# The delta rule's decay matrices: six tiles in the outputs' accumulators beside the pair of their own, in a hybrid attention layer

## The chip, the cores and the metric

The kernel runs on one core of a Trainium2 chip. The metric is device time in microseconds of one execution; the times of before are the median of three runs. Beside them stands one execution that was recorded by the hardware profiler. The kernel is written with a tile framework: tiles come from pools with a number of buffers each, the framework puts in the semaphore waits, and a scheduler that simulates the program (`schedule_with_timeline_sim=True`) decides in which order each engine gets its instructions. On the chip every engine then works through its list in that order.

## What is computed

One layer with 512 latent tokens and 256 context tokens, model width 1024: a half-step SwiGLU feed-forward block (FFN1), then two mixers side by side, neighbourhood attention with 8 heads of 64 and a bidirectional gated delta rule with 4 heads of 128, merged by gates, then a second feed-forward block (FFN2). The change is in the delta rule. Its core in the reference, for chunks of tokens:

```python
k, v, g, beta = chunk(k), chunk(v), jnp.cumsum(chunk(g), axis=-1), chunk(beta)
decay = jnp.exp(jnp.where(lower, g[..., :, None] - g[..., None, :], -jnp.inf))
k_beta = k * beta[..., None]
m = jnp.where(strict, jnp.einsum('...ik,...jk->...ij', k_beta, k) * decay, 0.0)
uw = lax.linalg.triangular_solve(jnp.eye(GDN_CHUNK, dtype=m.dtype) + m, rhs, left_side=True, lower=True, unit_diagonal=True)
...
# per chunk, state s:
v_new = u - w @ s;  s_next = s * g_tot + k_tail^T @ v_new
o = (q * exp(g)) @ s + ((q k^T) * decay) @ v_new
```

The decay matrix, the exponential of differences of a running sum, multiplies both products, k·k (before the triangular inverse) and q·k (for the outputs).

## The kernel before

The kernel works with chunks of 128 tokens: six steps `s` of the scan, of which 0 and 1 are the context's and 2 to 5 the latent tokens', in both directions at once. Two heads make a pair `p`, so a pair and a step hold four 128x128 matrices (two directions, two heads).

**Grams.** `gram(p, s, bd, g)` makes what one pair and step need. It takes a tile `Dt` of [128, 4, 128] (pool `gbase`, 2 buffers), loads the running sums `gcd` into it with one DMA from SyncE's queue (SP, L918), subtracts and masks with four instructions of VectorE (DVE, L921) and takes the exponential on ScalarE (ACT, L922). TensorE (PE) makes k·k in PSUM (`pq`, 2 buffers; every matmul of this part is issued by the helper at L857). Four DVE instructions make `Bt = pq * beta * Dt` (L927), and a DMA stores it to `bd` (L928). From step 2 on there is also the product q·k, from which DVE makes `At` (L931). For steps 4 and 5 the products come back from DRAM (`kq<-kqd`, L906), where steps 2 and 3 left them (L901, L902). The twelve grams are numbered here 0 to 11 in program order; four of them are a group, `grams(0)`, `grams(1)`, `grams(2)`.

**Inverses.** Behind each group stands `base_inverse`. It loads the diagonal 32x32 blocks of the group's sixteen matrices from `bd` (`Ltr` and `L`, L947; a copy on ACT, L948; a memset on GpSimd, L950), and inverts them in 31 steps, each a multiplication `bt` (L954) and a reduction into `Xt` (L955) on DVE. Here this is called the chain. Four DMAs write `Xt` to `rd` (L959). `inverse` reads these blocks back (`T<-rd`, L976), transposes them (L978, L979) and builds the inverses of 64x64 and 128x128 blocks with small matmuls (`pi`, L857). The scan's steps (`scan_step`) use them; from step 2 on they write the outputs to the accumulators `oacc0` and `oacc1`, one for each pair of heads, [128, 4, 2, 128] each (pool `gq`), which `gdn_out` reads at the end.

**Fill work.** Beside all this, PE has to multiply the latent tokens with further columns of `w_in`: matmuls into `pm` (L190 to L192, each weight split into `wh`, cast on ACT at L135, and `wl`, subtracted on DVE at L137, from `wr`, loaded at L172). Their results leave PSUM over ACT (`spill`, L605 to L609) and SP (L613). `turn` releases them at set rates behind the last matmul of the delta rule, by `tc.issue_after`. The attention that follows makes scores `sc` (L1240), transposes probabilities (`pt`, L1255), copies them on ACT (`pT`, L1257) and multiplies them with the values (`po`, L1266); the merge of the mixers fills PE in between, with `pm` matmuls as well.

The program order of the part that matters: some fill work, `grams(0)` with its chain, `grams(1)`, then the inverses of group 0 between the steps of group 1's chain, the scan's first steps, `grams(2)`, and so on.

Of the kernel before, what the change touches and what calls it, by code (L numbers as in the profile page):

```python
# [13 lines left out]
ALU = mybir.AluOpType  # L14
# [4 lines left out]
P = 128  # L19
# [39 lines left out]
def body(ctx, tc, I, out, dbg=None):  # L59
    nc = tc.nc  # L60
    V, S, G, T = nc.vector, nc.scalar, nc.gpsimd, nc.tensor
    dbg = dbg or {}

    def pool(name, side="left", space=None):
        kw = dict(name=name, bufs=1, reuse_waits="tile")
        if space is not None:
            kw["space"] = space
        else:
            kw["side"] = side
        g = tc.tile_pool(**kw)  # L70
        st = ExitStack()
        p = st.enter_context(g)
        return p, st.close
# [17 lines left out]
    ident = ident_t[:]  # L91
# [12 lines left out]
    def rsqrt_eps(sp, src, n, scale=None, eng=G):  # L104

        ve = tl(sp, [P, n], f"ve{n}", 4)
        if scale is None:
            marks["ve"] = eng.tensor_scalar(ve[:], src, EPS, None, op0=ALU.add).ins  # L108
        else:
            G.tensor_scalar(ve[:], src, scale, EPS, op0=ALU.mult, op1=ALU.add)  # L110
        rs = tl(sp, [P, n], f"rs{n}", 4)
        G.tensor_tensor(rs[:], ve[:], mhalf[:, 0:n], ALU.pow)  # L112
        return rs
# [508 lines left out]
    beta = tl(gd, [P, 2, 6, 4], "beta")  # L622
    gcum = tl(gd, [P, 2, 6, 4], "gcum")
# [223 lines left out]
    gq, close_gq = pool("gq")  # L847
    spool, done = [gq], [0]
    gb_, close_gb = pool("gbase", "right")
# [6 lines left out]
    def mm(*a, **k):  # L856
        last[0] = T.matmul(*a, **k).ins  # L857

    def mt(*a):
        last[0] = T.transpose(*a).ins  # L860
# [11 lines left out]
    def turn(kind, i):  # L872

        due[0] += RATE[kind][i]
        while due[0] >= 1:
            due[0] -= 1
            with tc.issue_after(last[0]):
                next(fills, None)

    def mats_of(s):  # L880
        return [(0, FWD_CH[s], 0), (0, FWD_CH[s], 1), (1, BWD_CH[s], 0), (1, BWD_CH[s], 1)]
# [6 lines left out]
    def products(p, s):  # L888
# [21 lines left out]
        if s >= 2:  # L910
            yield one(1, qT, 2)
            turn("g", s // 2)

    def gram(p, s, bd, g):

        mats = mats_of(s)
        Dt = tl(gb_, [P, 4, P], "Dt", 2)
        nc.sync.dma_start(Dt[:], bass.AP(gcd.tensor, gcd.offset + (4 * s + 2 * p) * P, [[0, P], [24 * P, 2], [1, 2 * P]]))  # L918
        for m, (d, c, i) in enumerate(mats):
            msk = cst[:, (C_MF if d == 0 else C_MB):][:, 0:P]  # L920
            V.scalar_tensor_tensor(Dt[:, m], Dt[:, m], gcum[:, d, s, 2 * p + i:2 * p + i + 1], msk, op0=ALU.subtract, op1=ALU.add)  # L921
        S.activation(Dt[:], Dt[:], AF.Exp)  # L922
        Bt, At = tl(gq, [P, 4, P], "Bt", NBT), None
        for n, t in enumerate(products(p, s)):
            if n == 0:
                for m, (d, c, i) in enumerate(mats):
                    V.scalar_tensor_tensor(Bt[:, m], t[m] if s == 1 else t[:, m], beta[:, d, s, 2 * p + i:2 * p + i + 1], Dt[:, m], op0=ALU.mult, op1=ALU.mult)  # L927
                nc.sync.dma_start(bass.AP(bd.tensor, bd.offset + g * MSTR, [[P, P], [4 * MSTR, 4], [1, P]]), Bt[:])  # L928
            else:
                At = tl(gq, [P, 4, P], "At", NAT)  # L930
                V.tensor_tensor(At[:], t[:], Dt[:], ALU.mult)  # L931
        return Bt, At
# [103 lines left out]
    def bc4(t, s, p):  # L1036

        return t[:, :, s, 2 * p:2 * p + 2, None].to_broadcast([P, 2, 2, P])

    def v4(t):  # L1040
        return t.rearrange("p (d i) c -> p d i c", d=2)

    oaccs = [tl(gq, [P, 4, 2, P], f"oacc{p}") for p in range(2)]

    def scan_step(p, s, Tt, At, Sst):
        cf, cb = FWD_CH[s], BWD_CH[s]
        mats = mats_of(s)
        oacc = oaccs[p]
        if Sst is not None:
            ks = tl(pgq, [P, 4, P], "pc", 2)  # L1050
            for m, (d, c, i) in enumerate(mats):
                mm(ks[:, m, :], kT[2 * p + i][:, c], Sst[:, m], start=True, stop=True)
            turn("s", s // 2)
            r = tl(gq, [P, 4, P], "r", 2)
            for m, (d, c, i) in enumerate(mats):
                V.scalar_tensor_tensor(r[:, m], ks[:, m], neg[:, d, s, 2 * p + i:2 * p + i + 1], vtok[2 * p + i][:, c], op0=ALU.mult, op1=ALU.add)
            rs = [r[:, m] for m in range(4)]
        else:
            rs = [vtok[2 * p + i][:, c] for (d, c, i) in mats]
        pv = tl(pgq, [P, 4, P], "pc", 2)  # L1060
        for m in range(4):
            mm(pv[:, m, :], Tt[m], rs[m], start=True, stop=True)
        turn("s", s // 2)
        vn = tl(gq, [P, 4, P], "vn", 2)
        V.tensor_tensor(v4(vn[:]), v4(pv[:]), bc4(beta, s, p), ALU.mult)
        Sn = None
        if s < 5:
            kt = tl(gq, [P, 4, P], "ktail")
# [12 lines left out]
        if s >= 2:  # L1081
            o1 = tl(pgq, [P, 4, P], "pc", 2)
            for m, (d, c, i) in enumerate(mats):
                mm(o1[:, m, :], qT[2 * p + i][:, c - 2], Sst[:, m], start=True, stop=True)
            turn("s", s // 2)
            ot = tl(gq, [P, 4, P], "otmp")
            V.tensor_tensor(v4(ot[:]), v4(o1[:]), bc4(eg, s, p), ALU.mult)
            o2 = tl(pgq, [P, 4, P], "pc", 2)
            for m in range(4):
                mm(o2[:, m, :], At[:, m], vn[:, m], start=True, stop=True)  # L1090
            turn("s", s // 2)
            if s < 4:
                V.tensor_tensor(oacc[:, cf - 2], ot[:, 0:2], o2[:, 0:2], ALU.add)
                V.tensor_tensor(oacc[:, cb - 2], ot[:, 2:4], o2[:, 2:4], ALU.add)
            else:
                V.tensor_tensor(ot[:], ot[:], o2[:], ALU.add)
                G.tensor_tensor(oacc[:, cf - 2], oacc[:, cf - 2], ot[:, 0:2], ALU.add)
                G.tensor_tensor(oacc[:, cb - 2], oacc[:, cb - 2], ot[:, 2:4], ALU.add)
        return Sn

    def gdn_out(p):

        oacc = oaccs[p]
        for t2 in range(2):
            o = oacc[:, 2 * t2:2 * t2 + 2].rearrange("p t i c -> p (t i) c")
            sq = tl(gq, [P, 4, P], "r", 2)
            S.activation(sq[:], o, AF.Square)
            ss = tl(gq, [P, 4], "ss", 2)
            V.tensor_reduce(ss[:], sq[:], AX, ALU.add)
            rs = rsqrt_eps(gq, ss[:], 4, 1.0 / 128.0)  # L1110
            V.tensor_tensor(o, o, rs[:, :, None].to_broadcast([P, 4, P]), ALU.mult)
        for i in range(2):
            ps = tl(pgq, [P, 4, P], "pc", 2)
            for t in range(4):
                mt(ps[:, t, :], oacc[:, t, i, :], ident)
            o = tl(gq, [P, 4, P], "vn", 2)[:].rearrange("p t c -> p (t c)")
            S.activation(o, ps[:].rearrange("p t c -> p (t c)"), AF.Copy, scale=nw[:, 0:1])
            nc.sync.dma_start(obd[2 * p + i], o)
# [11 lines left out]
    def step(gen, n=8):  # L1130
        for _ in range(n):
            next(gen, None)
# [4 lines left out]
    def scan_of(bi, j):  # L1137
        p = j % 2
        Sst[p] = scan_step(p, 2 * bi + j // 2, inv[(bi, j)], res[(bi, j)][1], Sst[p])
# [6 lines left out]
    step(base, 4)  # L1146
    inv_of(0, 1)
    step(base)
    scan_of(0, 0)
    scan_of(0, 1)  # L1150
    base = grams(2)
# [39 lines left out]
    for p in range(2):  # L1191
        gdn_out(p)
# [137 lines left out]
    for m in range(8):  # L1330
        wso.fill(min(4 + (m + 1) // 2, 7))
        gt, ps = gated("pa", gad, m, oah, oal)
# [230 lines left out]
    for t in range(4):  # L1563
        h = tl(lp, [P, D], "h4", 2)
        n, m = (512, D) if t < 3 else (D // PIECES, 512)
# [125 lines left out]
```

## Time and profile before

| | us |
|---|---|
| median of three runs (1529.55, 1523.28, 1527.39) | 1527.39 |
| the profiled execution | 1530.66 |
| its span in the trace | 1528.8 |
| mean granted clock of PE in it (1 is full speed) | 0.988 |
| first and last subtraction of a decay (L921) | 743.0, 860.6 |
| first and last exponential of a decay (L922) | 745.2, 861.0 |

The grams with their decays lie in about 118 us in the middle of the span. Times within the trace count from the span's start. In a row of the timeline the first number is the start, the second the duration, and a bracket at the end gives the idle time of that engine before the instruction and what ended it. In a view of waits the numbers are the total, the count and the longest. In the lines of windows the columns are the stretch, its length, the busy time (with the number of instructions) of PE, of its weight loads, DVE, ACT and GpSimd, then the granted clock, the busy share of the DMA engines and GB/s.

### The profile page before, as it was taken

The numbers are of one execution on the slowest core, as the hardware profiler recorded it, in microseconds if no ns is written. First come the engines' busy times: TensorE is split into PE (matmuls) and PEld (weight loads), VectorE is DVE, ScalarE is ACT, GpSimd is POOL, SyncE is SP. The second block draws the span as 40 slices with busy tenths as digits, with TensorE's granted clock in tenths as the row PEclk, the third lists the DMA queues.
The fourth block names the chain that finished last, engine by engine and source line by source line (L and its number), as shares of the span: only waits on it lengthen the run. The fifth ranks groups of instructions, "written<-read, shape, count | busy, mean of one in ns | idle before, by whom it ended". The sixth has DMA issues, their size and how long they took to land.

```text
span 1528.8 us, 23646 instructions
## 1 busy us (share of the span) xinstructions
PE 1462.6 (96%) x9221; PEld 1258.7 (82%) x9221; DVE 1050.0 (69%) x1792; ACT 605.4 (40%) x1005; POOL 226.8 (15%) x224
## 2 busy tenths in 40 slices
PE   6999999999999999999996899999999999999997
PEld 4779988888888887889875778867678999998886
DVE  8765942597554587768777895576669699886426
ACT  5444221322222255546543444266416444344310
POOL 0000000000000011323301001366421022220001
PEclk9999999999999999999998999999999999999999
DMA  9665742667454334222476634283353143333422
GB/s 370 207 237 180 222 142 97 211 213 260 168 192 146 130 112 137 87 90 79 141 216 180 172 99 122 69 284 117 91 174 138 56 139 102 106 110 139 138 83 83
DMA packets 107586, 230.72 MB, mean 151 GB/s; under 512 B 34177, under 2 KB 47825, under 8 KB 107473
## 3 DMA queue, kind: packets, MB, share of 16 engines
q1 hardware_dynamic: 105312, 221.79, 44.7%
q10 hardware_dynamic: 1586, 5.32, 0.9%
q0 software_dynamic: 576, 2.10, 0.4%
q8 instruction: 72, 1.18, 0.3%
q14 instruction: 40, 0.33, 0.1%
HBM read 206.33 MB, written 22.85 MB: 150 GB/s over the span
## 4 chain that ended last, share of the span: by engine, by line
PE 76%; DVE 10%; DMA 7%; issue 3%; ACT 2%; POOL 2%; SPq 0%; DVEq 0%; ACTq 0%; POOLq 0%
PE ps L209 19%; PE ps L190 8%; PE ps L192 8%; PE ps L191 8%; PE pm L190 5%; PE pm L192 5%; PE pm L191 5%; PE pc L857 2%; PE ps L1478 2%; PE ps L1480 2%; PE ps L1479 2%; DVE wl L137 2%; PE po L1266 1%; DMA T<-rd 1%; PE pt L1255 1%
## 5 line engine op out<-in xcount | busy, mean ns | idle before, releaser
L137 DVE TENSOR_TENSOR wl<-wr,wh 128x1024 fp32r<-128x1024 f32 (+1 forms) x215 | 263.0, 1228 | 195.1 <-ACT wh L135 194.3
L135 ACT CAST wh<-wr 128x1024 fp32r<-128x1024 f32 (+1 forms) x215 | 217.8, 1018 | 333.4 <-PE ps L209 105.0
L192 PE MATMUL ps<-uxh,wl 128*128 128x512 f32 (+1 forms) x496 | 179.6, 363 | 2.2 <-DVE wl L137 2.2
L191 PE MATMUL ps<-uxl,wh 128*128 128x512 f32 (+1 forms) x496 | 179.3, 363 | 0.8 <-DVE uxl L137 0.8
L190 PE MATMUL ps<-uxh,wh 128*128 128x512 f32 (+1 forms) x496 | 179.6, 365 | 0.0
L279 DVE SCALAR_TENSOR_TENSOR adap<-wr,crow 128x1024 f32<-128x1024 f32 x112 | 136.8, 1221 | 38.5 <-DMA wr<-in_w_adaT_dram 37.1
L112 POOL TENSOR_TENSOR rs<-ve,mhalf 128x1 f32<-128x1 f32 (+2 forms) x46 | 50.4, 1099 | 744.6 <-DVE ve L108 735.4
L190 PE MATMUL pm<-uxh,wh 128*128 128x512 f32 x320 | 133.0, 416 | 4.1 <-ACT spill L609 2.1
L192 PE MATMUL pm<-uxh,wl 128*128 128x512 f32 x320 | 128.2, 401 | 0.7 <-DVE wl L137 0.7
L191 PE MATMUL pm<-uxl,wh 128*128 128x512 f32 x320 | 127.8, 399 | 0.0
L192 PEld LDWEIGHTS ps<-uxh,wl 128*128 128x128 f32 x496 | 93.7, 189 | 17.9 <-DVE wl L137 3.3
L191 PEld LDWEIGHTS ps<-uxl,wh 128*128 128x128 f32 x496 | 94.0, 189 | 14.9 <-DVE uxl L137 1.0
L190 PEld LDWEIGHTS ps<-uxh,wh 128*128 128x128 f32 x496 | 93.4, 189 | 14.3 <-issue 0.8
L190 PE MATMUL ps<-uch,wh 128*128 128x256 f32 x352 | 98.6, 280 | 0.0
L192 PE MATMUL ps<-uch,wl 128*128 128x256 f32 x352 | 98.3, 279 | 0.0
L191 PE MATMUL ps<-ucl,wh 128*128 128x256 f32 x352 | 98.2, 279 | 0.0
L209 PE MATMUL ps<-wh,hx 128*128 128x512 f32 x352 | 94.8, 389 | 0.0
L209 PEld LDWEIGHTS ps<-wh,hx 128*128 128x128 f32 x352 | 65.9, 188 | 13.6
L190 PEld LDWEIGHTS pm<-uxh,wh 128*128 128x128 f32 x320 | 61.6, 193 | 16.3 <-ACT spill L609 3.0
L192 PEld LDWEIGHTS pm<-uxh,wl 128*128 128x128 f32 x320 | 61.7, 193 | 14.8 <-DVE wl L137 1.5
L191 PEld LDWEIGHTS pm<-uxl,wh 128*128 128x128 f32 x320 | 61.6, 192 | 10.6
L190 PEld LDWEIGHTS ps<-uch,wh 128*128 128x128 f32 x352 | 66.1, 188 | 0.6
(411 smaller groups left out, 3438.7 us busy)
## 6 DMA issues: line engine op xcount, KB each, us to landing
wr<-in_w_adaT_dram SPq DMA_DIRECT2D x88, 512.0 KB, 4.7
wr<-in_up_dram SPq DMA_DIRECT2D x80, 512.0 KB, 4.2
wr<-in_dn_dram SPq DMA_DIRECT2D x58, 512.0 KB, 3.5
wr<-in_win_dram SPq DMA_DIRECT2D x52, 512.0 KB, 3.9
rb<-in_up_dram SPq DMA_DIRECT2D x18, 512.0 KB, 3.7
wr<-in_w_o_dram SPq DMA_DIRECT2D x8, 512.0 KB, 4.0
ac<-in_up_dram SPq DMA_DIRECT2D x6, 512.0 KB, 5.2
Dt<-gcd SPq DMA_DIRECT2D x12, 256.0 KB, 5.1
```

The source lines that it names most:

```text
L112: G.tensor_tensor(rs[:], ve[:], mhalf[:, 0:n], ALU.pow)
L135: S.copy(hi, src)
L137: V.tensor_tensor(lo, src, hi.bitcast(F32), ALU.subtract)
L190: T.matmul(ps, a, uh[:, k, :], start=(k == 0), stop=False)
L191: T.matmul(ps, a, ul[:, k, :], start=False, stop=False)
L192: T.matmul(ps, b, uh[:, k, :], start=False, stop=(k == nk - 1))
L209: T.matmul(banks[t][d][:, c0:c1], a[:, sl], b[:, d * 512 + c0:d * 512 + c1], start=first and j == 0, stop=last and j == 2)
L279: V.scalar_tensor_tensor(pr[:], raw[:], 1.0, crow, op0=ALU.mult, op1=ALU.mult, accum_out=col[:, c:c + 1])
L857: last[0] = T.matmul(*a, **k).ins
L1478: T.matmul(ps[:], a, uh[:, k], start=k == 0, stop=False)
L1479: T.matmul(ps[:], a, ul[:, k], start=False, stop=False)
L1480: T.matmul(ps[:], b, uh[:, k], start=False, stop=k == 3)
```

## The change

Each gram takes its decay's tile from a list. Grams 0, 1 and 8 to 11 keep `Dt` with its two buffers. Grams 2, 3, 4, 5, 6 and 7 put theirs into the accumulators: `oacc0` and `oacc1`, formerly two tiles, are now four of half the size, `oacc0` to `oacc3` (the same bytes in all), and take the decays in the order 0, 1, 2, 3, 0, 1. The scan takes them as accumulators afterwards. For steps 4 and 5, grams 8 to 11, the four subtractions may not be issued before the last Bt instruction of the gram before (`tc.issue_after(bt_last[0])`). What a tile's name says of its use changes with it: `oacc` in a row on L927 is a decay now. Lines behind the change stand 6 lower at first (L921 is L927, L927 is L933, L931 is L937, L954 is L960, L959 is L965), and 10 lower in the attention (L1255 is L1265).

```diff
+    gram_n, bt_last = [0], [None]
     def gram(p, s, bd, g):
         mats = mats_of(s)
-        Dt = tl(gb_, [P, 4, P], "Dt", 2)
+        k = (None, None, 0, 1, 2, 3, 0, 1, None, None, None, None)[gram_n[0]]
+        gram_n[0] += 1
+        Dt = tl(gb_, [P, 4, P], "Dt", 2) if k is None else tl(gq, [P, 4, P], f"oacc{k}")
         nc.sync.dma_start(Dt[:], ...)
         for m, (d, c, i) in enumerate(mats):
-            V.scalar_tensor_tensor(Dt[:, m], Dt[:, m], gcum[...], msk, op0=ALU.subtract, op1=ALU.add)
+            with tc.issue_after(bt_last[0]) if s > 3 else nullcontext():
+                V.scalar_tensor_tensor(Dt[:, m], Dt[:, m], gcum[...], msk, op0=ALU.subtract, op1=ALU.add)
         S.activation(Dt[:], Dt[:], AF.Exp)
...
-                    V.scalar_tensor_tensor(Bt[:, m], ...)
+                    bt_last[0] = V.scalar_tensor_tensor(Bt[:, m], ...).ins
...
-    oaccs = [tl(gq, [P, 4, 2, P], f"oacc{p}") for p in range(2)]
+    oaccs = [[], []]
+    def out_of(p, c):
+        return oaccs[p][c // 2][:, 2 * (c % 2):2 * (c % 2) + 2]
...
     step(base)
+    for k in range(4):
+        oaccs[k // 2].append(tl(gq, [P, 4, P], f"oacc{k}"))
     scan_of(0, 0)
```

The scheduler's order moves with it, at three places. The first is DVE's list where the first two groups' Bt are made, up to the start of the first chain. Before (names with a number are one buffer's tile; `x4` is four instructions alike):

```order
L810 COPY vcs_6699<-pg_6696 128x256
L137 TENSOR_TENSOR wl_6823<-wr_6820,wh_6822 128x1024
L927 SCALAR_TENSOR_TENSOR Bt_6809<-pq_6810,beta_5004,Dt_6802 128x128 x4
L927 SCALAR_TENSOR_TENSOR Bt_6846<-pq_6810,beta_5004,Dt_6839 128x128 x4
L921 SCALAR_TENSOR_TENSOR Dt_6867<-Dt_6867,gcum_5005,cst_5002 128x128 x4
L137 TENSOR_TENSOR wl_6888<-wr_6885,wh_6887 128x1024
L921 SCALAR_TENSOR_TENSOR Dt_6904<-Dt_6904,gcum_5005,cst_5002 128x128 x4
L927 SCALAR_TENSOR_TENSOR Bt_6874<-pq_6875,beta_5004,Dt_6867 128x128 x4
L927 SCALAR_TENSOR_TENSOR Bt_6911<-pq_6875,beta_5004,Dt_6904 128x128 x4
L137 TENSOR_TENSOR wl_7069<-wr_7066,wh_7068 128x1024
L921 SCALAR_TENSOR_TENSOR Dt_7045<-Dt_7045,gcum_5005,cst_5002 128x128 x4
L921 SCALAR_TENSOR_TENSOR Dt_7135<-Dt_7135,gcum_5005,cst_5002 128x128 x4
```

And DVE at the same place with the change:

```order
L810 COPY vcs_6699<-pg_6696 128x256
L927 SCALAR_TENSOR_TENSOR oacc_1231_6865<-oacc_1231_6865,gcum_5005,cst_5002 128x128 x4
L927 SCALAR_TENSOR_TENSOR oacc_1238_6902<-oacc_1238_6902,gcum_5005,cst_5002 128x128 x4
L137 TENSOR_TENSOR wl_6821<-wr_6818,wh_6820 128x1024
L933 SCALAR_TENSOR_TENSOR Bt_6807<-pq_6808,beta_5004,Dt_6800 128x128 x4
L933 SCALAR_TENSOR_TENSOR Bt_6844<-pq_6808,beta_5004,Dt_6837 128x128 x4
L927 SCALAR_TENSOR_TENSOR oacc_1277_7043<-oacc_1277_7043,gcum_5005,cst_5002 128x128 x4
L927 SCALAR_TENSOR_TENSOR oacc_1293_7133<-oacc_1293_7133,gcum_5005,cst_5002 128x128 x4
L933 SCALAR_TENSOR_TENSOR Bt_6872<-pq_6873,beta_5004,oacc_1231_6865 128x128 x4
L137 TENSOR_TENSOR wl_6886<-wr_6883,wh_6885 128x1024
L933 SCALAR_TENSOR_TENSOR Bt_6909<-pq_6873,beta_5004,oacc_1238_6902 128x128 x4
L927 SCALAR_TENSOR_TENSOR oacc_1310_7232<-oacc_1310_7232,gcum_5005,cst_5002 128x128 x4
```

The decays of grams 2 and 3 now stand ahead of a weight split and of the Bt of grams 0 and 1, and those of grams 4 and 5 ahead of the Bt of grams 2 and 3; the decay of gram 6 (`oacc_1310`) and, a few rows on, that of gram 7 stand ahead of the chain, inside which they stood before, as did the first At (gram 4).

The second place is the queue of SP at the same time, before:

```order
L811 DMA vcd_4988<-vcs_6699 128x256
L613 DMA qad_4991<-spill_6763 128x512
L613 DMA kad_4992<-spill_6797 128x512
L172 DMA wr_7066<-in_win_dram 128x1024
L928 DMA bd_1221_6800<-Bt_6809 128x4x128
L918 DMA Dt_6867<-gcd_4994 128x2x256
L928 DMA bd_1221_6800<-Bt_6846 128x4x128
L918 DMA Dt_6904<-gcd_4994 128x2x256
```

And SP with the change:

```order
L811 DMA vcd_4988<-vcs_6699 128x256
L923 DMA oacc_1231_6865<-gcd_4994 128x2x256
L923 DMA oacc_1238_6902<-gcd_4994 128x2x256
L613 DMA qad_4991<-spill_6761 128x512
L923 DMA oacc_1277_7043<-gcd_4994 128x2x256
L923 DMA oacc_1293_7133<-gcd_4994 128x2x256
L613 DMA kad_4992<-spill_6795 128x512
L172 DMA wr_7064<-in_win_dram 128x1024
L934 DMA bd_1219_6798<-Bt_6807 128x4x128
L923 DMA Dt_7937<-gcd_4994 128x2x256
L934 DMA bd_1219_6798<-Bt_6844 128x4x128
L923 DMA Dt_7964<-gcd_4994 128x2x256
```

The loads of grams 2 to 5 stand ahead of the first Bt stores, and behind those stores come the loads of grams 8 and 9 (`Dt_7937`, `Dt_7964`) already; later, the load that stood between the chain's last steps and the rd writes is gone from there.

The third place is PE in the attention, some 200 us later, at a tile's transposes, before:

```order
L1255 MATMUL pt_9487<-ident_64,pr_9473 128x128 x4
L1240 MATMUL sc_9691<-kc_9675,qah_9664 128x256 x2
L1240 MATMUL sc_9691<-kch_9674,qa_9665 128x256 x2
L190 MATMUL pm_9712<-obh_9362,wh_9632 128x512
L191 MATMUL pm_9712<-obl_9363,wh_9632 128x512
L192 MATMUL pm_9712<-obh_9362,wl_9633 128x512
```

And PE with the change:

```order
L1265 MATMUL pt_9489<-ident_64,pr_9475 128x128 x4
L1250 MATMUL sc_9693<-ka_9672,qah_9666 128x256 x2
L1250 MATMUL sc_9693<-kah_9671,qa_9667 128x256 x2
L1250 MATMUL sc_9693<-kch_9676,qah_9666 128x256 x2
L1276 MATMUL po_9400<-pT_9487,vw_9438 64x128
L1276 MATMUL po_9400<-pT_9494,vw_9438 64x128
```

Here the products `po` follow their transposes after six score matmuls, where four of these and a run of merge matmuls stood between before.

More of the change, by code (lines that the diff above doesn't have):

```diff
@@ L920, in gram @@
             msk = cst[:, (C_MF if d == 0 else C_MB):][:, 0:P]
-            V.scalar_tensor_tensor(Dt[:, m], Dt[:, m], gcum[:, d, s, 2 * p + i:2 * p + i + 1], msk, op0=ALU.subtract, op1=ALU.add)
+            with tc.issue_after(bt_last[0]) if s > 3 else nullcontext():
+                V.scalar_tensor_tensor(Dt[:, m], Dt[:, m], gcum[:, d, s, 2 * p + i:2 * p + i + 1], msk, op0=ALU.subtract, op1=ALU.add)
         S.activation(Dt[:], Dt[:], AF.Exp)
@@ L926, in gram @@
                 for m, (d, c, i) in enumerate(mats):
-                    V.scalar_tensor_tensor(Bt[:, m], t[m] if s == 1 else t[:, m], beta[:, d, s, 2 * p + i:2 * p + i + 1], Dt[:, m], op0=ALU.mult, op1=ALU.mult)
+                    bt_last[0] = V.scalar_tensor_tensor(Bt[:, m], t[m] if s == 1 else t[:, m], beta[:, d, s, 2 * p + i:2 * p + i + 1], Dt[:, m], op0=ALU.mult, op1=ALU.mult).ins
                 nc.sync.dma_start(bass.AP(bd.tensor, bd.offset + g * MSTR, [[P, P], [4 * MSTR, 4], [1, P]]), Bt[:])
@@ L1047, in scan_step @@
         mats = mats_of(s)
-        oacc = oaccs[p]
         if Sst is not None:
@@ L1092, in scan_step @@
             if s < 4:
-                V.tensor_tensor(oacc[:, cf - 2], ot[:, 0:2], o2[:, 0:2], ALU.add)
-                V.tensor_tensor(oacc[:, cb - 2], ot[:, 2:4], o2[:, 2:4], ALU.add)
+                V.tensor_tensor(out_of(p, cf - 2), ot[:, 0:2], o2[:, 0:2], ALU.add)
+                V.tensor_tensor(out_of(p, cb - 2), ot[:, 2:4], o2[:, 2:4], ALU.add)
             else:
                 V.tensor_tensor(ot[:], ot[:], o2[:], ALU.add)
-                G.tensor_tensor(oacc[:, cf - 2], oacc[:, cf - 2], ot[:, 0:2], ALU.add)
-                G.tensor_tensor(oacc[:, cb - 2], oacc[:, cb - 2], ot[:, 2:4], ALU.add)
+                for c, o in ((cf - 2, ot[:, 0:2]), (cb - 2, ot[:, 2:4])):
+                    G.tensor_tensor(out_of(p, c), out_of(p, c), o, ALU.add)
         return Sn
     def gdn_out(p):
-        oacc = oaccs[p]
         for t2 in range(2):
-            o = oacc[:, 2 * t2:2 * t2 + 2].rearrange("p t i c -> p (t i) c")
+            o = oaccs[p][t2][:]
             sq = tl(gq, [P, 4, P], "r", 2)
@@ L1114, in gdn_out @@
             for t in range(4):
-                mt(ps[:, t, :], oacc[:, t, i, :], ident)
+                mt(ps[:, t, :], out_of(p, t)[:, i], ident)
             o = tl(gq, [P, 4, P], "vn", 2)[:].rearrange("p t c -> p (t c)")
```

## The prediction

> **What bounds the kernel now.** I read the page's first lines and its chain that ended last, and then the waits of TensorE (PE) around the inverses.
>
> ```profile
> span 1528.8 us, 23646 instructions
> PE 1462.6 (96%) x9221; PEld 1258.7 (82%) x9221; DVE 1050.0 (69%) x1792; ACT 605.4 (40%) x1005; POOL 226.8 (15%) x224
> PE 76%; DVE 10%; DMA 7%; issue 3%; ACT 2%; POOL 2%; SPq 0%; DVEq 0%; ACTq 0%; POOLq 0%
> ...
> PE pi L857 <- DMA T<-rd: 13.0, 2, 12.4
> PE pi L857 <- DVE Y L1025: 3.5, 2, 2.8
> PE pc L857 <- DVE r L1056: 2.3, 2, 1.2
> PE pm L190 <- ACT spill L609: 2.1, 2, 1.5
> ```
>
> PE is busy in 96% of the span, so a change can gain at most where PE stands still. Between 725 and 1010 us, which holds the whole delta rule up to attention, one hole outweighs all others: 12.4 us of waiting for `T<-rd`, the first base inverse coming back from DRAM. The rest are pieces of under 3 us. So the question is when that T lands, and whether PE gets through its other work sooner or later.
>
> The stretches around the hole, each with the busy time of PE, its weight loads, VectorE (DVE), ScalarE (ACT) and GpSimd, the granted clock, the DMA share and GB/s, and then the rows of PE in time:
>
> ```profile
> 780.00:790.00 10.00, 8.14 (x35) 6.20 (x34) 6.58 (x27) 3.98 (x6) 0.00 (x0) 0.92 0.68 195
> 790.00:800.00 10.00, 10.00 (x48) 8.35 (x47) 8.62 (x25) 2.55 (x4) 0.00 (x0) 0.91 0.58 186
> 820.00:830.00 10.00, 0.00 (x0) 0.00 (x0) 4.13 (x21) 0.95 (x2) 1.16 (x6) 0.62 0.86 191
> ...
> 777.92 0.50 PE L190 MATMUL pm<-uxh,wh 128*128 128x512 f32 x1 [0.58 <-ACT spill L609]
> 779.00 0.50 PE L192 MATMUL pm<-uxh,wl 128*128 128x512 f32 x1 [0.35 <-DVE wl L137]
> 786.72 0.50 PE L190 MATMUL pm<-uxh,wh 128*128 128x512 f32 x1 [1.53 <-ACT spill L609]
> 787.78 0.50 PE L192 MATMUL pm<-uxh,wl 128*128 128x512 f32 x1 [0.33 <-DVE wl L137]
> 812.20 1.05 PE L857 MATMUL pq<-qT,kT 128*128 128x128 f32 x8
> 818.32 0.39 PE L192 MATMUL pm<-uxh,wl 128*128 128x512 f32 x1
> 831.15 0.68 PE L857 MATMUL pi<-T,Bt 32*32 32x32 f32 x32 [12.44 <-DMA T<-rd]
> ```
>
> PE runs out of fill work at 818.71 (818.32 + 0.39) and resumes at 831.15. What T waits for is a chain on DVE and then SyncE's queue (SP):
>
> ```profile
> 776.25 0.16 DVE L954 TENSOR_TENSOR bt<-L,Xt 128x2 f32<-128x2 f32 x1 [3.36 <-POOL L L950]
> 783.28 0.88 DVE L921 SCALAR_TENSOR_TENSOR Dt<-Dt,gcum,cst 128x128 f32<-128x128 f32 x3 [3.00 <-DMA Dt<-gcd]
> 794.74 1.14 DVE L921 SCALAR_TENSOR_TENSOR Dt<-Dt,gcum,cst 128x128 f32<-128x128 f32 x4 [1.11 <-DMA Dt<-gcd]
> 807.59 1.14 DVE L921 SCALAR_TENSOR_TENSOR Dt<-Dt,gcum,cst 128x128 f32<-128x128 f32 x4 [0.77 <-DMA Dt<-gcd]
> 817.40 0.69 DVE L955 TENSOR_REDUCE Xt<-bt 128x16 f32<-128x512 f32 x1
> 823.07 1.14 DVE L921 SCALAR_TENSOR_TENSOR Dt<-Dt,gcum,cst 128x128 f32<-128x128 f32 x4 [3.84 <-DMA Dt<-gcd]
> ...
> 817.95 0.43 SPq L918 DMA_DIRECT2D Dt<-gcd  x1
> 820.06 4.31 SPq L959 DMA_DIRECT2D rd<-Xt  x4
> 826.42 2.02 SPq L976 DMA_DIRECT2D T<-rd  x4
> ```
>
> The 31 steps of the triangular inversion run from 776.25 to 818.09 (817.40 + 0.69). Then come four writes of rd, four reads of T, and PE: 831.15 − 818.09 = 13.06 us from the chain's end to PE. Inside the chain DVE stood still three times for a decay's DMA, 3.00 + 1.11 + 0.77 = 4.88 us: with two `Dt` buffers, a gram's load starts only when the gram two before has read its decay for the last time.
>
> **The change part by part.** Its unit costs come from the view of the tile Dt:
>
> ```profile
> L921 DVE SCALAR_TENSOR_TENSOR Dt<-Dt,gcum,cst x48: 340/346/1397, 743.0 to 860.6; 128x128 f32<-128x128 f32 x48
> L922 ACT ACTIVATE Dt<-Dt x12: 626/632/634, 745.2 to 861.0; 128x512 f32<-128x512 f32 x12
> L931 DVE TENSOR_TENSOR At<-pq,Dt x4: 680/682/692, 776.5 to 816.1; 128x512 f32<-128x512 f32 x4
> DMA to landing us min/median/max: 4.0/5.1/5.6
> ```
>
> No instruction is added or dropped: 12 loads, 48 subtractions and 12 exponentials remain. They move.
>
> *Ahead of the chain.* Four loads now go out one behind another, before any Bt is made, where two stood interleaved with the Bt stores.
>
> ```profile
> 748.47 0.38 SPq L811 DMA_DIRECT2D vcd<-vcs  x1
> 754.69 0.50 SPq L918 DMA_DIRECT2D Dt<-gcd  x1
> ...
> 753.11 2.16 DVE L927 SCALAR_TENSOR_TENSOR Bt<-pq,beta,Dt 128x128 f32<-128x128 f32 x8
> 760.22 1.14 DVE L921 SCALAR_TENSOR_TENSOR Dt<-Dt,gcum,cst 128x128 f32<-128x128 f32 x4 [4.95 <-DMA Dt<-gcd]
> 763.47 2.15 DVE L927 SCALAR_TENSOR_TENSOR Bt<-pq,beta,Dt 128x128 f32<-128x128 f32 x8
> 758.58 0.39 PE L192 MATMUL pm<-uxh,wl 128*128 128x512 f32 x1
> ```
>
> Behind the vcd store at 748.47 they are issued from about 748.9 to 751.3, at 0.5 us each with one other load between, and land 4.0 to 5.6 us later. Against that, DVE now meets the new decays (`oacc0`, `oacc1`) ahead of a weight split (`wl`) and of the Bt of grams 0 and 1, and runs its list in order. If the first lands at 753.5, I lay the rows end to end: two grams' decays 2.3, `wl` 1.1, eight Bt 2.1, two more decays 2.2, four Bt 1.1, `wl` 1.1, four Bt 1.1, which ends at 764.5. Before it ended at 765.62 (763.47 + 2.15). So the wait of 4.95 us is traded for work that was done inside it. The Bt of gram 3 sets the chain's start through its store and the load of L; the start moves by −1 to +1 us, and I take **0**. Queued behind the new wait is `wl`: by the same count it is ready at 757, and PE's first use of it is at 758.58, so it just fits. If the loads land 2 us later, PE stands about half a microsecond.
>
> *Inside the chain.* The three waits go: −4.88 us. The decays of grams 6 and 7 (2 × 1.14) and the product At of gram 4 (0.68) go ahead of the chain: −2.96. The decays of gram 8 stay inside it, near its end. Sum −7.84, so the chain would end at 810.25. A bound from the other side: the last At reads a product that PE makes at 812.20 + 1.05 = 813.25. PE must reach it sooner. It does so by its stalls of 0.58 + 0.35 + 1.53 + 0.33 = 2.79 us, which stand behind ACT and DVE, and ACT was itself held by a late decay:
>
> ```profile
> 784.60 0.63 ACT L922 ACTIVATE Dt<-Dt 128x512 f32<-128x512 f32 x1 [6.27 <-DVE Dt L921]
> 786.07 0.59 ACT L609 ACTIVATE spill<-pm 128x512 f32<-128x512 f32 x1
> ```
>
> The exponential at 784.60 waited 6.27 us for the decay that DVE had got late, and the spill behind it on ACT is what PE then waited for at 786.72. Behind these stalls the granted clock fell, 0.92 and 0.91 in the two windows; lost are about 10 × (0.08 + 0.09) = 1.7 us. With stalls and dip gone PE is there 4.5 us sooner, the product is ready at 808.8 and does not bind; with neither gone it binds and the chain ends at about 814.6 (813.25, the product At and the last reduction, 0.68 each), a gain of 3.5. Ends: −3.5 and −7.84, and I take **−7.8**, since the row of 784.60 names a decay as the cause.
>
> *From the chain's end to T.* One Dt load of 0.43 us goes ahead of the loads of L and the rd writes no longer; the rd writes took 4.31 for four. Ends 0 and −2 (the rd writes at the 2.02 us that four T reads took); I take **−0.4**. PE's own fill work ends about 4.5 sooner, so the hole shrinks only from 12.4 to 12.4 − (7.8 + 0.4 − 4.5) = 8.7; the time that is won is T's, 8.2.
>
> *Given back later.* Gram 9's decays lay in the idle 3.84 us before 823.07, beside PE's hole; by the new bound they stand in the second chain, behind the last Bt of gram 8: **+1.1**, four of 346 ns less what overlaps. Ends −0.8 (a later load's wait that shrinks) and +1.1.
>
> *Attention.* The order differs once more 200 us later: fewer score and projection matmuls stand between a transpose of the probabilities and the products with them.
>
> ```profile
> PE po L1266 <- ACT pT L1257: 4.0, 5, 1.9
> ...
> 1034.88 0.90 PE L1266 MATMUL po<-pT,vw 128*64 128x128 f32 x5 [1.88 <-ACT pT L1257]
> ```
>
> Before, this wait took 4.0 us in 5 times over the whole span. Ends: −2 (some of it gone) and +4 (as much again). I take **+0.6**.
>
> Sum: −7.8 − 0.4 + 1.1 + 0.6 = **−6.5 us**. The profiled execution took 1530.66, its span 1528.8 and 1.86 around it; 1530.66 − 6.5 = 1524.2. It lies 3.27 above the median of the three runs, 1527.39, and against that the forecast is 1520.9, rounded to **1521**.
>
> [...] The rows first: in the windows with the stalls of 1.53 and 0.33 us the clock granted was 0.92 and 0.91, and in the empty window 0.62. [...]
>
> **The rivals.**
> 1. *The product binds.* ACT's stall has another cause (its spills wait for PE as well), PE gains nothing, and the chain ends only 3.5 us sooner. For it: the last At really stands behind PE. Against it: the 6.27 us row. −3.5 gives 1523.9.
> 2. *More goes.* T lands up to 9.8 us sooner (−7.84 − 2), the given-back terms are none, and the dip that follows the hole shortens with it: −9 to −10, about 1517.5. For it: the rd writes at twice the time of the T reads. Against it: they are different transfers.
> 3. *Slower: attention's order.* Products right behind their transposes wait for ACT's copy of the probabilities, 1.88 us as in the row of 1034.88. At 5 to 8 places that is 9.4 to 15 against −6.5: +3 to +8.5, 1530 to 1536. It decides from 4 places on (7.5 us). Against it: only 5 such waits in the whole trace of before, with a mean of 0.8.
> 4. *Nothing comes of it.* Only the place of a wait changes: the four loads land late, the chain starts 5 us later. 1526 to 1529. For it: at 86% DMA share the queues are near full in places; against it: the loads landed within 5.6 us everywhere.
>
> **How the numbers follow.** Forecast (1518.5 to 1523.5) 0.45; product binds (1524) 0.20; more (1517.5) 0.22; attention (1530 to 1536) 0.08; nothing 0.05. A measurement of this kernel tells about 0.5% from no change, 7.6 us, so faster means below 1519.8. The larger case lies below it, and a quarter of the forecast's range: 0.22 + 0.12 = 0.34. Above 1535 lies only the end of rival 3, taken at 0.05 with its upper half. The rest, 0.61, is the same. The range, 1514 to 1529, holds all but rival 3 and the far end of rival 2: the larger case at −10 is 1517.4, and 3 us below it are for the spread of the runs shown, 1523.28 to 1529.55 before.
>
> **What would show it.** Right: no wait of DVE for a decay between the chain's first and last step; a chain of about 34 us in place of 41.8; PE's wait for `T<-rd` at 8 to 9 us; no dip of the clock between 780 and 800. Wrong: a chain that starts over 2 us later, a last At that waits for PE, or waits of `po` for `pT` well above 4 us.

## The result, and the profile after

The changed kernel takes 1537.34 us (median of six runs, 1533.79 to 1538.69) against 1527.67 us of before: a ratio of 1.0063, interval 1.0045 to 1.008. That is slower by 0.6%, and outside the forecast's range. The profiled execution took 1533.79 us, 3.1 above before's 1530.66, where the medians lie 9.7 apart: it is the fastest of its six runs, and before's lies above all six of its own (1523.28 to 1529.55). So one profile against one profile understates the loss, and below stages are averaged over the profiles of several kernels.

The page of after, its busy line and the engines of the chain that ended last; then PE's waits between 725 and 1010 us:

```profile
span 1532.0 us, 23643 instructions
PE 1467.1 (96%) x9221; PEld 1264.5 (83%) x9221; DVE 1051.1 (69%) x1792; ACT 606.9 (40%) x1005; POOL 227.9 (15%) x224
PE 80%; DVE 10%; DMA 4%; issue 2%; ACT 1%; POOL 1%; SPq 1%; DVEq 0%; POOLq 0%; ACTq 0%
...
PE pi L857 <- DMA T<-rd: 11.0, 3, 10.1
PE pi L857 <- DVE Y L1031: 4.9, 3, 2.4
PE pc L857 <- DVE r L1065: 1.7, 3, 0.9
```

The hole before the first inverse is smaller, 10.1 in place of 12.4 us, and the same work of PE takes more busy time, 1467.1 in place of 1462.6. The stretches that the prediction watched, the first and the last step of the first chain on DVE, and PE's first use of T:

```profile
780.00:790.00 10.00, 10.00 (x54) 8.55 (x53) 9.38 (x31) 2.47 (x4) 0.00 (x0) 1.00 0.74 233
790.00:800.00 10.00, 10.00 (x50) 8.43 (x49) 9.59 (x23) 3.93 (x6) 0.00 (x0) 1.00 0.67 230
...
776.25 0.15 DVE L960 TENSOR_TENSOR bt<-L,Xt 128x2 f32<-128x2 f32 x1
...
810.21 0.68 DVE L961 TENSOR_REDUCE Xt<-bt 128x16 f32<-128x512 f32 x1
...
824.16 0.70 PE L857 MATMUL pi<-T,Bt 32*32 32x32 f32 x32 [10.09 <-DMA T<-rd]
```

Inside the chain this came as forecast: DVE is 94 and 96% busy in the two windows, it waits for no decay, the granted clock is 1.00 in both, and the chain lasts 34.6 us. The chain ends at 810.89 (forecast 810.25, before 818.09), and T is used at 824.16, 7.0 us sooner. But 2.4 us of this lead were there before the grams' part began, where the two kernels have the same order on every engine; the vcd store on SP and the first decay on DVE, with the change, are the anchors (before: 748.47 in the prediction, and 743.0):

```profile
746.03 0.38 SPq L811 DMA_DIRECT2D vcd<-vcs  x1
740.51 3.23 DVE L927 SCALAR_TENSOR_TENSOR Dt<-Dt,gcum,cst 128x128 f32<-128x128 f32 x8
```

Counted from the first decay, T comes 4.6 us sooner and the chain starts 2.4 us later (35.7 us in place of 33.3). The rest of the time went behind T. The first starts of four kinds of matmul cut the rest of the program into stages: the first inverse (`pi`), attention (`sc`), the merge of the mixers (`pm<-oah`), and the projection behind it (`yh`). Before, then after:

```profile
L857 PE MATMUL pi<-T,Bt x288: 191/212/267, 831.2 to 957.6; 32*32 32x32 f32 x96, 64*64 64x64 f32 x48
L1240 PE MATMUL sc<-kah,qah x32: 283/383/579, 994.0 to 1077.8; 64*128 64x256 f32 x32
L190 PE MATMUL pm<-oah,wh x32: 389/389/500, 1093.5 to 1118.8; 128*128 128x512 f32 x32
L209 PE MATMUL ps<-wh,yh x64: 389/389/397, 1119.5 to 1164.0; 128*128 128x512 f32 x64
...
L857 PE MATMUL pi<-T,Bt x288: 191/212/267, 824.2 to 952.8; 32*32 32x32 f32 x96, 64*64 64x64 f32 x48
L1250 PE MATMUL sc<-kah,qah x32: 278/384/579, 989.2 to 1077.5; 64*128 64x256 f32 x32
L190 PE MATMUL pm<-oah,wh x32: 387/389/628, 1093.2 to 1123.3; 128*128 128x512 f32 x32
L209 PE MATMUL ps<-wh,yh x64: 389/389/397, 1124.0 to 1168.9; 128*128 128x512 f32 x64
```

The lead, with those 2.4 us in it, is 7.0 us at the first inverse, 4.8 at the attention, 0.3 at the merge, and at the projection the changed kernel is 4.5 us behind. The loss has three places, two of them where the change has no line.

### The profile page after: what moved, and what is told of

Same layout as the page of the kernel before. It is cut to its first block, busy times and chain, and to the rows that moved or that the text cites. A ratio compares the mean times of both kernels' runs of the same rounds, so it can differ in the third digit from the quotient of the medians.

```text
span 1532.0 us, 23643 instructions
## 1 busy us (share of the span) xinstructions
PE 1467.1 (96%) x9221; PEld 1264.5 (83%) x9221; DVE 1051.1 (69%) x1792; ACT 606.9 (40%) x1005; POOL 227.9 (15%) x224
## 4 chain that ended last, share of the span: by engine, by line
PE 80%; DVE 10%; DMA 4%; issue 2%; ACT 1%; POOL 1%; SPq 1%; DVEq 0%; POOLq 0%; ACTq 0%
PE ps L209 19%; PE ps L190 9%; PE ps L192 9%; PE ps L191 9%; PE pm L190 5%; PE pm L192 5%; PE pm L191 5%; PE ps L1490 3%; PE ps L1489 3%; PE ps L1488 3%; PE pc L857 2%; DVE wl L137 2%; PE po L1276 1%; DVE bt L960 1%; PE pt L1265 1%
## 5 line engine op out<-in xcount | busy, mean ns | idle before, releaser
L112 POOL TENSOR_TENSOR rs<-ve,mhalf 128x1 f32<-128x1 f32 (+2 forms) x46 | 50.5, 1101 | 745.2 <-DVE ve L108 742.3
L192 PE MATMUL ps<-uch,wl 128*128 128x256 f32 x352 | 98.3, 279 | 0.0
L192 PEld LDWEIGHTS pm<-uxh,wl 128*128 128x128 f32 x320 | 60.8, 190 | 14.2 <-DVE wl L137 1.4
```

What stands on the lines that cost most here:

```text
L192: T.matmul(ps, b, uh[:, k, :], start=False, stop=(k == nk - 1))
```

## The experiments

The merge was the plainest. Rows of ACT (the weights' casts), then of PE, in the changed kernel:

```profile
1094.59 2.00 ACT L135 CAST wh<-wr 128x1024 fp32r<-128x1024 f32 x2
1100.38 2.09 ACT L135 CAST wh<-wr 128x1024 fp32r<-128x1024 f32 x3 [3.78 <-DMA wr<-in_w_o_dram]
...
1101.99 0.50 PE L190 MATMUL pm<-oah,wh 128*128 128x512 f32 x1 [3.03 <-ACT wh L135]
1105.22 0.79 PE L192 MATMUL pm<-oah,wl 128*128 128x512 f32 x1 [1.97 <-DVE wl L137]
```

And ACT at the same place before:

```profile
1098.54 1.14 ACT L135 CAST wh<-wr 128x512 fp32r<-128x512 f32 x2 [1.73 <-PE pm L191]
1100.56 1.04 ACT L135 CAST wh<-wr 128x1024 fp32r<-128x1024 f32 x1 [0.88 <-DMA wr<-in_w_o_dram]
```

At this place one row of ACT's order has moved, and its split on DVE with it. It is the cast of a `w_o` weight (1024 columns, needed after the merge). Before it stands behind two casts of `w_pa` weights (512 columns, needed at once), now ahead of them:

```
before  wh_10585 wh_10641 (w_o) | wh_10591 wh_10616 (w_pa) | wh_10697 (w_o)
after   wh_10587 wh_10643 (w_o) | wh_10699 (w_o) | wh_10593 wh_10618 (w_pa)
```

ACT stands for 3.78 us until the `w_o` load lands and only then gets to the two `w_pa` casts behind it, and PE waits for them.

**How the orders were held.** The scheduler's order can be imposed by edges between an engine's instructions that hold their order and add no wait. So a kernel can have the delta rule of one version and the order of the other behind it. `ORDER` is a table that lists, for each engine, the program positions in the sequence of issue:

```diff
+    at0 = len(nc.cur_bb.bb.instructions)
...
+    for e, text in ORDER.items():
+        mine = [i for i in traced if i.engine == getattr(mybir.EngineType, e)]
+        want = [n for r in text.split(",") for n in range(int(r.split("-")[0]), int(r.split("-")[-1]) + 1)]
...
+        for u, v in zip(want, want[1:]):
+            tc.add_manual_dep(mine[v], mine[u].name, mybir.DependencyInfo(mybir.DependencyClass.NoSync, mybir.DependencyReason.DATA), reason="issue_after")
```

`at0` is the program position from which the order is held: the attention's for the first six kernels and the last but one, an earlier one where said. A kernel with nothing but its own whole order held was not run; that the edges cost nothing by themselves is taken from the kernels that have them, which lie on both sides of before.

**The changed kernel with the old order behind the delta rule.** [`at0` at the attention, table of before]

> The delta rule as changed; from the attention's first instruction to the end every engine's instructions in the order of before. Theory A (the decays' places gain about 4.8 us by the end of the delta rule, and what was lost is the order that the scheduler chose behind it): the gain stays, about 1527.5 - 4.8 = 1522.7 us, the attention about 4 to 5 us earlier than before to its end. Theory B (an earlier delta rule collides with what follows, whatever the order: loads, clock): the gain is lost in the attention as in the changed kernel, 1527 to 1537 us.

Measured: 1529.82 us, ratio to before 1.0013 (0.9998 to 1.0027). The number lies in theory B's span, 7 us above theory A's, but B's place is wrong: by the stages below the attention takes as long as before, and the gain is lost ahead of it. The downstream order accounts for about 7.5 us of the 9.7, and the gain of the first chain does not reach the attention.

**The kernel of before with the new order behind the delta rule.** [the same edit in before, table of after]

> The delta rule as before; from the attention on every engine in the order of the changed kernel. Theory A: the downstream loss alone, at least the 7.9 us that the two profiles show between the end of the delta rule and the end (from 4.8 ahead to 3.1 behind), 1535 to 1542 us. Theory B: no loss, since the order costs nothing by itself, about 1527.5 us.

1535.32 us, ratio 1.0043 (1.0026 to 1.006). The order alone costs some 7 us, with no decay moved: theory A on this point.

**One cast put back, in the changed kernel; one cast put ahead, in before.** One entry of ACT's and one of DVE's table moves:

```diff
-    "Activation": "...,111,116,121,112,114,110,..."
+    "Activation": "...,111,116,112,114,121,110,..."
-    "DVE": "...,104,111,95,99,98,101,96,..."
+    "DVE": "...,104,95,99,98,101,111,96,..."
```

> The changed kernel with its whole downstream order held as it is, but for one weight of w_o: its cast on ScalarE and its split on VectorE stand behind those of the two w_pa weights again, as before. Theory A: PE's waits of 3.03 us for the cast and 1.97 for the split after it go; the gain is the 4.7 us lost between 1094 and 1124 us, 1537.3 - 4.7 = 1532.6 us. Theory B: the wait moves to another load and nothing is won, about 1537 us.

> The kernel of before with its own downstream order held, but for that one cast and split of w_o, which stand ahead of those of the two w_pa weights. Theory A: 4.7 us slower, about 1532.2 us, with PE waiting some 3 us for the cast behind the load of w_o. Theory B: no change, 1527.5 us.

1531.02 us, ratio 1.0026 (1.0013 to 1.004), against 1.0063 of the changed kernel; and 1531.66 us, 1.0036 (1.0023 to 1.0048): theory A in both. With the cast back PE's wait for the cast is gone, but 3.1 us of waits for splits stay in the merge, so its stage wins 3.0 us there and not 4.7; the medians differ by 6.3, and the profile, of an execution of 1534.95 us, does not show where the rest was won. Before with the one cast ahead shows the same two waits of PE (its line numbers are 8 higher, for the table):

```profile
1099.07 0.50 PE L198 MATMUL pm<-oah,wh 128*128 128x512 f32 x1 [2.92 <-ACT wh L143]
1102.30 0.80 PE L200 MATMUL pm<-oah,wl 128*128 128x512 f32 x1 [1.98 <-DVE wl L145]
```

One cast and one split, out of some 24,000 instructions, cost just under 0.4%: shown by doing it and by undoing it.

**What gives back the first chain's gain.** Two kernels take the change apart, both with the old order from the attention on: the places without the bound, and the bound alone in before.

```diff
-            with tc.issue_after(bt_last[0]) if s > 3 else nullcontext():
-                V.scalar_tensor_tensor(Dt[:, m], ...)
+            V.scalar_tensor_tensor(Dt[:, m], ...)
```

> The decays of grams 2 to 7 in the accumulators, without the bound of the third group; from the attention on every engine in the order of before (as in the run with the old order, 1529.8 us). Theory A (the bound gives back what the places win: it put decays of the third group into the second chain, 1.7 us longer there, and the third chain 3.4 longer): about 1529.8 - 5 = 1525 us, second chain about 48.7 us as before. Theory B (the gain is lost behind the first inverse whatever the bound, because VectorE and PE are full there): 1529 to 1530 us.

> The kernel of before with the bound alone: the decays of grams 8 to 11 may not be issued before the last Bt of the gram before; from the attention on in the order of before. Theory A: slower by 2 to 5 us, 1530 to 1533 us, first chain as long as before (41.4 us), second and third longer. Theory B: about as before, 1527 to 1529 us.

1526.01 us, ratio 0.9991 (0.9976 to 1.0007), and 1529.82 us, 1.0006 (0.9992 to 1.002). Each lies between its two theories and reaches unity with its interval. Without the bound the changed tiles are 3.8 us faster between medians; the bound alone costs before about 1 us, with an interval that holds no change. The chains give no simple account either: with the bound alone the second and third take 51.8 and 47.6 us (before 48.2 and 45.2), and without it the places still have 50.5 and 49.2. The next pair holds the order from an earlier position, `inv_of(0, 0)`, the first inverse: the places without the bound with the order of before from there on, and the reverse, before's tiles with the order of the changed kernel from there on.

> The decays of grams 2 to 7 in the accumulators, no bound, and every instruction from the first inverse to the end, on every engine, in the order of before: only the part up to the end of the first chain differs from before. Theory A (the new order of what follows gives the gain back): first chain about 36 us, second and third as before (48.7 and 45.0), the end of the delta rule 5 us earlier, about 1527.9 - 5 = 1523 us. Theory B (full engines): the second and third chain grow all the same by 1.7 and 3.4 us, no gain, 1527 to 1530 us.

> The counterpart: decays in the pair of tiles as before, but every instruction from the first inverse to the end, on every engine, in the order of the changed kernel (with the bound). Theory A: the loss of the order alone, behind the first inverse as well: 1535.3 (new order from the attention on) + 5 = about 1540 us. Theory B: about 1535 us, as with the new order from the attention on alone.

1524.38 us, ratio 0.9975 (0.9966 to 0.9985), and 1544.0 us, 1.0099 (1.0081 to 1.0117). The whole new order without the new places is the slowest kernel of all, 4 us above its theory A. The new places with the whole old order are faster than both kernels. For its stages the same program was run once more:

> The same program as the run with the places and the old order from the first inverse on, for its profile. Theory A: about 1524 us again; first chain about 36 us, second and third within 1 us of before's 48.7 and 45.0; the end of the delta rule 4 to 6 us earlier than before. Theory B (the second and third chain grow whatever the order): second over 50, third over 47.

1525.23 us, ratio 0.9982 (0.9971 to 0.9993). Its three chains on DVE, first step and last, and PE's first inverse; then, of before, the end of the second chain and the first and last step of the third, and the third of before with the new order:

```profile
780.86 0.15 DVE L967 TENSOR_TENSOR bt<-L,Xt 128x2 f32<-128x2 f32 x1
813.41 0.69 DVE L968 TENSOR_REDUCE Xt<-bt 128x16 f32<-128x512 f32 x1
826.16 0.16 DVE L967 TENSOR_TENSOR bt<-L,Xt 128x2 f32<-128x2 f32 x1 [0.44 <-POOL L L963]
870.80 0.69 DVE L968 TENSOR_REDUCE Xt<-bt 128x16 f32<-128x512 f32 x1
875.85 0.16 DVE L967 TENSOR_TENSOR bt<-L,Xt 128x2 f32<-128x2 f32 x1 [2.11 <-POOL L L963]
919.69 0.68 DVE L968 TENSOR_REDUCE Xt<-bt 128x16 f32<-128x512 f32 x1
829.15 0.31 PE L865 MATMUL pi<-T,Bt 32*32 32x32 f32 x2 [10.67 <-DMA T<-rd]
...
871.85 0.69 DVE L955 TENSOR_REDUCE Xt<-bt 128x16 f32<-128x512 f32 x1
876.64 0.16 DVE L954 TENSOR_TENSOR bt<-L,Xt 128x2 f32<-128x2 f32 x1 [2.37 <-POOL L L950]
921.18 0.68 DVE L955 TENSOR_REDUCE Xt<-bt 128x16 f32<-128x512 f32 x1
...
879.97 0.16 DVE L962 TENSOR_TENSOR bt<-L,Xt 128x2 f32<-128x2 f32 x1 [4.54 <-POOL L L958]
928.42 0.68 DVE L963 TENSOR_REDUCE Xt<-bt 128x16 f32<-128x512 f32 x1
```

With the old order the third chain takes 919.69 + 0.68 − 875.85 = 44.5 us, as before (45.2), and the second 45.3, less than before (48.2); with the new order and before's tiles the third takes 49.1, though it starts latest of all, at 879.97. So it is the order that stretches it, not an earlier start. The first chain is down to 33.2 us (before 41.8), but it starts 4.6 us later (780.86 in place of 776.25), T comes only 2.0 us sooner than before, and 15.1 us behind its chain in place of 13.1: in the order of its program SP issues two loads of L and a Dt load between the writes of rd and T's reads. In before's trace these took SP 1.47 and 0.43 us, ahead of the writes. The attention starts 1.7 us sooner than before, not the 4 to 6 that theory A asked for.

The attention alone was told apart by the new order in before with the cast at its old place:

> The delta rule as before, from the attention on the order of the changed kernel, but for the one cast and split of w_o, which stand where before had them. Theory A (the loss behind the delta rule has two parts, the cast with 3.8 us and the attention's order with the rest): 1535.3 - 3.8 = about 1531.5 us. Theory B (the cast was all of it): about 1528 us.

1531.62 us, ratio 1.0022 (1.001 to 1.0035): as theory A. Last, a try to keep both the early T and the old order, by holding the order only from `base = grams(2)` on:

> The decays of grams 2 to 7 in the accumulators, no bound; the inverses of the first group are free to move, and from the third group's grams on every engine follows the order of before. By the stages of the runs so far: from the first decay to the first inverse on PE about 83 us as in the changed kernel (86.3 with the old order from the first inverse on, 89.3 before), from there to the attention 163 to 166 us, the rest as before. Theory A (each stage's time goes with its own order): about 1527.5 - 6 + 2 = 1523.5 us. Theory B (whatever the first inverse wins, VectorE and PE lose before the attention): 1526 us or more.

1525.2 us, ratio 0.9987 (0.9976 to 0.9997). It lies between its theories. By the stages below T gains nearly as much as hoped, 84.2 us in its stage, and the next stage is 167.7, longer than the 163 to 166 expected; but the execution of that profile took 1529.69 us, 4.5 above the median.

**The stages.** From the first starts as quoted above, in us, one profile each; "first" runs from the first decay to the first inverse. Ahead of the first decay the kernels with before's tiles take 741.8 us on average and the others 741.6.

| kernel | first | inverse to attention | attention | merge | rest |
|---|---|---|---|---|---|
| before | 88.2 | 162.8 | 99.5 | 26.1 | 409.3 |
| before, new order from attention | 90.7 | 162.1 | 103.4 | 30.4 | 405.7 |
| before, one cast ahead | 90.7 | 160.9 | 97.6 | 30.7 | 408.0 |
| before, attention's order new | 90.2 | 162.7 | 102.4 | 25.8 | 408.8 |
| before, bound alone | 88.0 | 165.3 | 99.2 | 26.1 | 409.3 |
| before, new order from inverse | 88.1 | 170.9 | 102.4 | 31.1 | 407.3 |
| changed | 83.6 | 165.0 | 104.1 | 30.8 | 408.0 |
| changed, old order from attention | 83.2 | 168.6 | 100.1 | 25.9 | 407.7 |
| changed, one cast back | 85.3 | 172.9 | 100.5 | 27.8 | 406.2 |
| places, no bound | 82.8 | 166.2 | 97.0 | 25.6 | 409.8 |
| places, old order from inverse | 86.3 | 163.2 | 98.3 | 26.0 | 407.5 |
| places, old order from third group | 84.2 | 167.7 | 96.9 | 26.1 | 409.6 |

The columns are compared by what the kernels have in common there. First: the six with before's tiles 89.3 on average (88.0 to 90.7), the first four with the new places 83.7 (82.8 to 85.3), −5.6. Inverse to attention: the five in the old order, without the bound, 162.3 (160.9 to 163.2), the four in the changed kernel's order 169.4 (165.0 to 172.9), +7.1; the three others have orders of their own there and lie between, 165.3 to 167.7. Attention: seven old 98.4, five new 102.6, +4.2. Merge: eight with the cast behind 26.2, four with it ahead 30.8, +4.6. Rest, in the groups of the attention: −1.5. The sum is +8.8 us, against 9.7 between the medians. The second term is the least certain: four kernels with one order in that stage differ by 7.9 us among themselves.

## Why the prediction was wrong, point by point

- **Ahead of the chain (0, ends −1 and +1): wrong, and hidden.** The chain starts at 776.25 in both profiles, but counted from the first decay it starts 2.4 us later; over the six and the four profiles of the table 36.4 us in place of 33.7, +2.7. Gram 3's Bt do end sooner, as worked out: 760.98 + 1.11 − 740.51 = 21.6 us behind the first decay, before 22.7. But SP waits longer for the store of Bt to land before it loads the blocks of L (between 735 and 780 us, before and after):

```profile
SPq L947 <- DMA bd<-Bt: 2.7, 1, 2.7
SPq L953 <- DMA bd<-Bt: 5.1, 2, 3.3
```

  From the store of gram 3's Bt to that load it is 6.4 us (762.12 to 768.55) in place of 4.4 (765.64 to 770.08). Why the store takes longer to land was not tried.
- **Inside the chain (−7.8): right in kind, a little less in size.** The three waits for decays went and the product did not bind; the chain is 7.2 us shorter in the two profiles, 6.4 over the table's. The stalls did not go: 0.58 and 0.35 us of PE at the chain's start became 1.94 and 0.57, and only the later two, 1.53 and 0.33, are gone. The dip between 780 and 800 us went in this execution (granted 1.00, before 0.92 and 0.91); with the old order from the attention on, the same delta rule had one at 781 us (0.50 from there to 783).
- **From the chain's end to T (−0.4, ends 0 and −2): not decided by two profiles.** It took 13.27 us in place of 13.06 in them, and 1.9 us less over the table's. The hole was 10.1 us, not 8.7.
- **Luck.** That the chain's end (810.89) and T came so near to the forecast is owed to the 2.4 us by which this execution was ahead already. T's 8.2 us sooner are 5.6 over the table's profiles.
- **Given back later (+1.1, ends −0.8 and +1.1): this is the step that failed most.** I priced one gram's decays in the second chain and took the rest of the delta rule to move with T. It does not: from the first inverse to the attention the stage grew by 7.1 us, more than the first stage won. That stage (PE's busy time in the second place behind the window, the granted clock behind POOL) in before, in before with the new order from the inverse on, in the changed kernel, and in the changed kernel with the one cast back:

```profile
831.15:993.98 162.83, 153.73 (x1534) 127.86 (x1534) 120.46 (x312) 65.50 (x144) 27.07 (x44) 0.97 0.39 116
829.92:1000.79 170.87, 157.39 (x1534) 130.44 (x1534) 122.94 (x323) 66.14 (x145) 27.30 (x44) 0.96 0.38 110
824.16:989.17 165.01, 154.07 (x1535) 128.06 (x1536) 122.00 (x317) 66.19 (x145) 26.98 (x44) 0.98 0.38 114
825.72:998.64 172.92, 158.72 (x1534) 131.31 (x1534) 121.97 (x316) 65.93 (x145) 27.25 (x44) 0.95 0.37 109
```

  PE stands still for 9.1, 13.5, 10.9 and 14.2 us, and is busy for up to 5 us longer with the same matmuls where the granted clock is lower (158.72 us at 0.95, before 153.73 at 0.97). The order of the engines behind the first inverse, which the change shifted in many small places (the bound among them), does it with before's tiles as well: by the medians the kernel of before takes 1535.32 us with the new order from the attention on and 1544.0 with it from the inverse on, 8.7 us more. With the new places the same step back to the old order, without the bound, wins 5.4 (1529.82 to 1524.38). Which of these rows costs how much stays open: bound alone and places alone are each near nothing by their intervals, and the run that held the order from the third group on gained in the first stage, by its one profile, about what it lost in the next.
- **Attention (+0.6, ends −2 and +4): its size was wrong, +4.2, and its kind.** I looked for waits of `po` for `pT`. These went from 4.0 to 2.1 us over the span. PE's idle time hardly changed, but the clock did:

```profile
994.00:1094.00 100.00, 92.41 (x731) 69.84 (x731) 63.87 (x92) 62.49 (x141) 63.75 (x41) 0.97 0.50 171
989.00:1093.00 104.00, 95.80 (x730) 73.11 (x728) 64.73 (x92) 62.90 (x141) 63.40 (x41) 0.92 0.50 164
995.00:1098.00 103.00, 93.92 (x733) 71.49 (x733) 63.62 (x92) 63.00 (x141) 62.74 (x41) 0.95 0.49 166
```

  These are before, the changed kernel, and before with the attention's new order: idle 7.6, 8.2 and 9.1 us, granted 0.97, 0.92 and 0.95, busy up to 3.4 us longer for the same matmuls. One of the five profiles in the new order (the cast put back) had 0.97 here as well, so it is a likelihood and not a rule. That this order costs time is shown in before (1.0022); whether and how it brings the lower clock about was not tried by itself.
- **The merge: put at nothing, +4.6.** I compared the orders of PE there, which are equal, and not those of ACT and DVE, where one row decided 4.6 us. The order was said to move at three places; by the names in the two traces it moves at far more, in some 30 stretches of DVE's list and a dozen of SP's between the first inverse and the attention alone.
- **The rivals.** The slower one named the attention's order and 1530 to 1536 us, by a mechanism that did not happen, and had 0.08. The range ended at 1529: the failure of several terms at once, mostly a scheduler's side effects, was not priced.

## What to carry to other kernels

Where a scheduler sets the order, a change's price is its own effect plus that of every row that moves behind it: here −5.6 us in its own stage and some +14 behind it, by the means of the table, mostly rows that the change doesn't name. Compare the orders on every engine, weight casts and loads included, down to the end, and price each pair of rows whose data come at different times. Holding the old order behind an edit tells the two apart, and the places with the old order kept were the fastest kernel here, about 0.2% ahead of before in both of its measurements (0.9975 and 0.9982).

## What the runs showed of the hardware

The granted clock fell behind PE's stalls in one run and stayed at 1.00 behind like stalls in another. In the changed kernel PE stood 1.94 and 0.57 us at the first chain's start, and in the run with the old order from the attention on 1.85 and 0.57, at the same matmuls. Behind them, in this order, stand the windows of the one and of the other:

```profile
777.09 0.50 PE L190 MATMUL pm<-uxh,wh 128*128 128x512 f32 x1 [1.94 <-ACT spill L609]
781.00:785.00 4.00, 4.00 (x23) 3.44 (x23) 3.83 (x14) 1.17 (x2) 0.00 (x0) 1.00 0.86 295
...
778.11 0.50 PE L198 MATMUL pm<-uxh,wh 128*128 128x512 f32 x1 [1.85 <-ACT spill L617]
781.00:783.00 2.00, 2.00 (x6) 1.53 (x5) 1.86 (x10) 0.00 (x0) 0.00 (x0) 0.50 0.82 235
784.00:787.00 3.00, 3.00 (x19) 2.61 (x18) 2.73 (x10) 0.59 (x1) 0.00 (x0) 1.00 0.82 255
```

Granted was 1.00 in the one; in the other it was 0.50 from 781 to 783 us and 1.00 again from 784 to 787. In the attention of the changed kernel, idle times of 2.18 and 0.83 us were followed by nine microseconds at 0.50, with PE 98% busy in them:

```profile
1031.73 0.66 PE L1234 MATMUL pt<-ident,vst 128*128 128x128 f32 x4 [2.18 <-ACT pT L1267]
1033.22 1.12 PE L1276 MATMUL po<-pT,vw 128*64 128x128 f32 x8 [0.83 <-DVE vw L1235]
...
1029.00:1033.00 4.00, 1.21 (x10) 0.73 (x7) 2.18 (x3) 2.94 (x8) 2.90 (x3) 0.93 0.76 278
1033.00:1042.00 9.00, 8.78 (x56) 7.00 (x56) 2.83 (x6) 3.76 (x11) 3.50 (x3) 0.50 0.12 31
```

What decides whether the clock falls behind such stalls, no run here shows. Nor was it tried why runs of one kernel differ by several microseconds (before: 1523.45 to 1532.55 in 31 runs).
